# Per-channel constants issued from ScalarE's DMA queue instead of SyncE's in the opening of a one-layer hybrid trunk

## The chip, the cores and the metric

The kernel runs on one core of a Trainium2 chip. A core has five engines that run side by side: TensorE (matrix products, PE in the profile, with its weight loads listed as PEld), VectorE (DVE), ScalarE (ACT), GpSimd (POOL) and SyncE (SP). Each engine takes its own instructions in order. Data moves between the DRAM and the on-chip memory by DMAs. SP, ACT and POOL can issue a DMA; the issue occupies the issuing engine's queue (SPq, ACTq, POOLq in the profile) for a moment, and the data arrives, or "lands", later.

The metric is the device time of one execution in microseconds (us), the median of several runs.

## The reference, cut to what matters

One layer of a streaming-encoder trunk, on a sequence of 512 tokens with 1024 channels, in 32-bit floats. The part in which the change lies is the very beginning: the input's normalisation and the first columns of the input projection, which feed the first branch gate.

```
h     = rms_norm(x, norm_mix)                       # 512 x 1024
proj  = h @ w_in                                    # to 8192 columns
u_pool, u_lru, q, k, v, g_logits = split(proj)
gates = sigmoid(g_logits + b_gate)                  # three gates of 1024 channels
y_pool, y_lru, y_sb = pooling, recurrence, attention mixers
merged = sum over the three branches of gate * (y @ w_branch)
x = x + merged @ w_out
x = x + (silu(h2 @ w_gate) * (h2 @ w_up)) @ w_down  # h2 = rms_norm(x, norm_ffn)
```

`rms_norm` divides each token by its root mean square and multiplies each channel by its entry in `norm_mix`.

## The kernel before, in words

Channels lie on the 128 partitions and tokens along the free dimension. The input comes transposed, `xt`, as eight tiles of 128 channels by 512 tokens, called here xt0 to xt7. Nearly every product is made from three: an operand is split into a rounded part ("hi") and its remainder ("lo"), and hi x hi, hi x lo and lo x hi are summed, so a splitting pair of instructions on ACT (hi) and DVE (lo) stands before every weight tile and every activation tile that TensorE reads.

All the small per-channel vectors (norm weights, gate biases, convolution weights, the constants of the recurrence and so on) are packed by the host into one array `vecs`, 128 partitions by 114 numbers. One DMA brings it into the tile `vt`, where every user takes its column with `vcol(name, i)`. The first users are the splitting of the first input tiles (`make_h`, L433 to 439), which scales by a column of `norm_mix`, and `lru_constants` (L539 to 560), a chain of small VectorE instructions with one on GpSimd, whose results are wanted much later.

The opening runs like this. While nothing has landed, TensorE runs nine products on a constant tile (`warm_ps`, L422), whose results nobody reads. SP issues the DMA of `vt` (L447), then per k the tile xt_k (`load_xt`, L431), and the matching piece of weights. The first weight tile `raw0` is loaded in two halves of 256 KB (L450): the half for k = 0 from ACT's queue, the half for k = 1 from SP's. Each half is split by VectorE alone (cast on L451, remainder on L452). `make_h(k)` then makes hi of the scaled input on ACT (L437) and lo on DVE (L438); both read xt_k and `vt`. Later weight tiles of this stage come through `emit_next`, which issues a 512 KB DMA on SP (L117) and splits on ACT (L110) and DVE (L111).

TensorE's first real work is the loop on L701: for each k, twelve products of 128 x 128 by 512 into four accumulators `ps_gate`: four with the hi weights and hi input, four with the lo weights and hi input, four with the hi weights and lo input. For eight k these are 96 products. They need, in this order: hi weights and hi input, lo weights, lo input. After them come the rest of the first gate, the recurrence's columns, the attention, the branch products, the output product and the feed-forward network, all run by TensorE one after another in a fixed order.

The order of the instructions on each engine is laid down when the program is built, by a scheduler that sorts by priorities and its own estimates of when operands come; the hardware then follows this order. A DMA has one of eight completion counters, given out in turn, and the eighth DMA after it waits on its queue until the counter's last DMA has landed.

Of the kernel before, what the change touches and what calls it, by code (L numbers as in the profile page):

```python
# [66 lines left out]
def layer_kernel(ctx: ExitStack, tc: tile.TileContext, x, xt, vecs, w_in, w_qkv7, w_gate7, w_pool, w_rg, w_ig,  # L67
                 w_branch, w_br7, w_out, w_fg, w_fu, w_fd, w_fd7, out):
    nc = tc.nc
# [22 lines left out]
    def cols(ap, k0, nk, c0, nc_):  # L92
        return ap[k0 * P:(k0 + nk) * P, c0:c0 + nc_].rearrange("(k p) c -> p k c", p=P)
# [198 lines left out]
    vt = cst.tile([P, NV], F32, tag="vt", name="vt")  # L292
# [115 lines left out]
    with ExitStack() as first:  # L408
# [21 lines left out]
        def load_xt(k):  # L430
            nc.sync.dma_start(xts[k], xt[k * P:(k + 1) * P, :])  # L431

        def make_h(k):  # L433
            t = t4([2, S], f"hu{k}", F32R)
            hh, hl = t[:, 0, :], t[:, 1, :]
            gcol = vcol("norm_mix", k)
            act(hh, xts[k], AF.Copy, scale=gcol)  # L437
            dve.scalar_tensor_tensor(hl, xts[k], gcol, hh.bitcast(F32), ALU.mult, ALU.subtract)  # L438
            hu.append((hh, hl))
# [4 lines left out]
        raw0 = wp.tile([P, 2, 512], F32, tag="raw", name="raw0")  # L444
        ready["first", 0] = hi0, lo0
        src0 = cols(w_in, 0, 2, 5120, 512)
        nc.sync.dma_start(vt, vecs)  # L447
        for k in range(2):
            load_xt(k)
            (nc.sync if k else nc.scalar).dma_start(raw0[:, k, :], src0[:, k, :])  # L450
            dve.tensor_copy(hi0[:, k, :], raw0[:, k, :])  # L451
            dve.tensor_tensor(lo0[:, k, :], raw0[:, k, :], hi0[:, k, :].bitcast(F32), ALU.subtract)  # L452
            make_h(k)
# [802 lines left out]
    with ExitStack() as ffn:  # L1256
# [18 lines left out]
        for c in range(4):  # L1275
# [10 lines left out]
            for j in range(2):  # L1286
                k = 2 * c + j
# [382 lines left out]
```

## Time and profile before

| what | value |
| --- | --- |
| median of 3 runs | 901.03 us (900.64 to 901.3) |
| the profiled execution's own time | 900.73 us |
| its span in the profile | 899.0 us |
| granted TensorE clock, share of full | 1.0 |
| busy: TensorE products | 893.4 us (99%) |
| busy: VectorE | 732.3 us (81%) |
| busy: ScalarE | 523.2 us (58%) |
| busy: GpSimd | 86.3 us (10%) |

The profile gives for each engine how long it was busy, and for each wait which other engine or DMA ended it. A row of the timeline has a start in us from the beginning of the span, a duration, the engine, the source line, the operation with its output and inputs, and a count when several neighbours were merged. "SPq" and "ACTq" are the queues of SP and ACT, whose rows are the issues of DMAs, not the transfers. "To landing" is the time from the start of an issue to the last arrival. The profiled execution's time is 1.73 us longer than its span and 0.30 us below the median of the runs.

### The profile page before, as it was taken

How to read it: one execution, taken by the hardware profiler on the slowest of the kernel's cores; microseconds unless marked ns; L12 is line 12 of the kernel's file. 1: busy time of each engine (PE TensorE's matmuls, PEld its weight loads, DVE VectorE, ACT ScalarE, POOL GpSimd, SP SyncE). 2: the span in 40 equal slices, each digit the busy share in tenths (PEclk: the TensorE clock that was granted, in tenths of full speed). 3: DMA queues.
4: the chain of work that ended last, by engine and by line, in shares of the span. 5: the costliest groups of instructions: out<-in, count | busy, mean ns of one | idle time of the engine just before them, and what ended most of it. 6: DMA issues, size and time to landing. Idle time of an engine off the chain costs nothing.

```text
span 899.0 us, 14052 instructions
## 1 busy us (share of the span) xinstructions
PE 893.4 (99%) x5491; PEld 794.2 (88%) x5491; DVE 732.3 (81%) x922; ACT 523.2 (58%) x722; POOL 86.3 (10%) x126
## 2 busy tenths in 40 slices
PE   9999999999999999999999999999999999999998
PEld 6888778788899888888888988889999999989998
DVE  7897897988786599967887696699888888799764
ACT  7554989556856556555664544454555555664532
POOL 1110002232332101000001100000000000101200
PEclk9999999999999999999999999999999999999999
DMA  9585347789682785734736865245543333866842
GB/s 337 147 303 156 115 127 215 234 286 242 181 260 71 233 235 190 220 118 141 223 91 152 184 177 170 94 131 152 141 117 95 111 102 125 225 167 122 180 99 94
DMA packets 116579, 151.98 MB, mean 169 GB/s; under 512 B 8096, under 2 KB 90016, under 8 KB 116512
## 3 DMA queue, kind: packets, MB, share of 16 engines
q1 hardware_dynamic: 104416, 107.30, 37.7%
q0 software_dynamic: 11952, 43.52, 20.6%
q8 instruction: 43, 0.70, 0.3%
q10 hardware_dynamic: 144, 0.26, 0.1%
q14 instruction: 24, 0.20, 0.1%
HBM read 130.61 MB, written 18.87 MB: 166 GB/s over the span
## 4 chain that ended last, share of the span: by engine, by line
PE 95%; DVE 2%; ACT 2%; issue 1%; DMA 0%; SPq 0%; DVEq 0%; ACTq 0%
PE ps_y L287 11%; PE ps_x L287 8%; PE ps_q L798 7%; PE ps_dy L287 5%; PE ps_dx L287 4%; PE ps_br L278 3%; PE ps_br L279 3%; PE ps_br L280 3%; PE ps_gate L701 2%; PE ps_bY L1238 2%; PE ps_gy L287 2%; PE ps_gate L280 2%; PE ps_bX L1238 2%; PE ps_gx L287 2%; PE ps_gate L279 2%; PE ps_gate L278 2%
## 5 line engine op out<-in xcount | busy, mean ns | idle before, releaser
L110 ACT ACTIVATE whi<-raw 128x1024 fp32r<-128x1024 f32 x73 | 77.2, 1058 | 85.3 <-PE ps_out L279 17.0
L111 DVE TENSOR_TENSOR wlo<-raw,whi 128x1024 fp32r<-128x1024 f32 x73 | 89.1, 1220 | 32.9 <-ACT whi L110 32.9
L111 DVE TENSOR_TENSOR wlo<-qw,whi 128x1024 fp32r<-128x1024 f32 x48 | 58.6, 1222 | 20.8 <-ACT whi L110 20.5
L110 ACT ACTIVATE whi<-qw 128x1024 fp32r<-128x1024 f32 x48 | 50.8, 1057 | 33.1 <-PE ps_q L798 18.6
L1403 ACT ACTIVATE wh_S<-w_S 128x1024 fp32r<-128x1024 f32 x36 | 38.2, 1064 | 35.5 <-PE ps_y L287 22.4
L1404 DVE TENSOR_TENSOR wl_S<-w_S,wh_S 128x1024 fp32r<-128x1024 f32 x36 | 43.8, 1220 | 6.2 <-ACT wh_S L1403 6.2
L1403 ACT ACTIVATE wh<-w 128x1024 fp32r<-128x1024 f32 x27 | 28.8, 1066 | 30.3 <-issue 11.9
L1494 POOL DMA_DIRECT2D dw<-in_w_down_dram x16 | 13.5, 846 | 325.9 <-DVE wl L1404 248.2
L1404 DVE TENSOR_TENSOR wl<-w,wh 128x1024 fp32r<-128x1024 f32 x27 | 32.9, 1220 | 10.0 <-ACT wh L1403 10.0
L1403 ACT ACTIVATE whdS<-dw 128x1024 fp32r<-128x1024 f32 x16 | 17.0, 1064 | 24.4 <-PE ps_dy L287 13.2
L1404 DVE TENSOR_TENSOR wldS<-dw,whdS 128x1024 fp32r<-128x1024 f32 x16 | 19.6, 1224 | 12.9 <-ACT whdS L1403 12.9
L1054 DVE TENSOR_TENSOR_SCAN E<-K,ahead 128x512 f32<-128x512 f32 (+3 forms) x32 | 25.3, 812 | 4.4 <-ACT K L1050 4.4
L278 PE MATMUL ps_br<-yHH,whi 128*128 128x512 f32 x64 | 25.3, 395 | 0.0
L278 PE MATMUL ps_lru<-HH,whi 128*128 128x512 f32 x64 | 25.2, 394 | 0.0
L278 PE MATMUL ps_br<-yph,whi 128*128 128x512 f32 x64 | 25.2, 394 | 0.0
L278 PE MATMUL ps_pool<-HH,whi 128*128 128x512 f32 x64 | 25.2, 393 | 0.0
L279 PE MATMUL ps_br<-ypl,whi 128*128 128x512 f32 x64 | 25.0, 391 | 0.0
L280 PE MATMUL ps_gate<-HH,wlo 128*128 128x512 f32 x64 | 25.0, 391 | 0.0
L278 PE MATMUL ps_gate<-HH,whi 128*128 128x512 f32 x64 | 25.0, 391 | 0.0
L280 PE MATMUL ps_br<-yph,wlo 128*128 128x512 f32 x64 | 25.0, 391 | 0.0
L279 PE MATMUL ps_br<-yHL,whi 128*128 128x512 f32 x64 | 25.0, 390 | 0.0
L279 PE MATMUL ps_pool<-HL,whi 128*128 128x512 f32 x64 | 25.0, 390 | 0.0
(717 smaller groups left out, 3426.3 us busy)
## 6 DMA issues: line engine op xcount, KB each, us to landing
raw<-in_w_in_dram SPq DMA_DIRECT2D x31, 512.0 KB, 5.2
qw<-in_w_qkv_dram SPq DMA_DIRECT2D x24, 512.0 KB, 6.8
w<-in_w_ffn_gate_dram SPq DMA_DIRECT2D x36, 256.0 KB, 4.1
w<-in_w_ffn_up_dram SPq DMA_DIRECT2D x36, 256.0 KB, 4.6
raw<-in_w_branch_dram SPq DMA_DIRECT2D x16, 512.0 KB, 4.4
dw<-in_w_down_dram POOLq DMA_DIRECT2D x16, 512.0 KB, 6.3
qw<-in_w_qkv_dram POOLq DMA_DIRECT2D x12, 512.0 KB, 7.6
qd<-r POOLq DMA_DIRECT2D x12, 512.0 KB, 7.2
```

The source lines that it names most:

```text
L110: act(hi, raw, AF.Copy)
L111: dve.tensor_tensor(lo, raw, hi.bitcast(F32), ALU.subtract)
L278: nc.tensor.matmul(ps, lh, rh, start=start, stop=False, skip_group_check=skip)
L279: nc.tensor.matmul(ps, lh, rl, start=False, stop=False, skip_group_check=skip)
L280: nc.tensor.matmul(ps, ll, rh, start=False, stop=stop, skip_group_check=skip)
L287: nc.tensor.matmul(o, a_[a][:, w, k, :], b_[b][:, k, :], start=first and n == k == 0, stop=last and n == 2 and k == 3, skip_group_check=True)
L701: nc.tensor.matmul(pss[n // 2][n % 2], w[:, k % 2, n * P:(n + 1) * P], hu[k][x_], start=k == 0 and w is wh and x_ == 0, stop=k == KT - 1 a ...
L798: nc.tensor.matmul(ps[:, a, :], b_[:, k, ts_], a_[:, kk, :], start=first and n == k == 0, stop=n == 2 and k == 3, skip_group_check=True)
L1054: dve.tensor_tensor_scan(E[:, c0:c0 + n][:, ::-1], K[:, c0 + 1:c0 + n + 1][:, ::-1], ahead[:, S - n:][:, ::-1], 0.0, ALU.mult, ALU.add)
L1238: nc.tensor.matmul(o, ah[x_][:, w, k, :], b[k][y_], start=first_ and n == k == 0, stop=n == 2 and k == 3, skip_group_check=True)
L1403: act(h, src, AF.Copy)
L1404: dve.tensor_tensor(l, src, h.bitcast(F32), ALU.subtract)
```

## The change

The DMA that loads `vt` is taken from the head of SP's queue and placed on ACT's queue, behind the DMA of the first half of `raw0`. SP's queue then begins with xt0. No tile, size or computation is changed.

```diff
         src0 = cols(w_in, 0, 2, 5120, 512)
-        nc.sync.dma_start(vt, vecs)
         for k in range(2):
             load_xt(k)
             (nc.sync if k else nc.scalar).dma_start(raw0[:, k, :], src0[:, k, :])
+            if k == 0:
+                nc.scalar.dma_start(vt, vecs)
             dve.tensor_copy(hi0[:, k, :], raw0[:, k, :])
             dve.tensor_tensor(lo0[:, k, :], raw0[:, k, :], hi0[:, k, :].bitcast(F32), ALU.subtract)
             make_h(k)
```

In the built program the order on TensorE and GpSimd is the same as before. On ACT one DMA issue stands between the first DMA and the loading of the activation table. On SP the first DMA is gone. On VectorE the first thirty or so instructions are in another order: before, three small instructions of `lru_constants` (L540, L544, L545) stand ahead of the cast of the first half of `raw0` (L451); after, the cast and the remainder (L451, L452) come first, then two of the small ones, then lo of xt0 (L438), the cast of the second half, lo of xt1, and the remainder of the second half. From the last steps of the `lru_constants` chain on, some forty instructions in, VectorE's order is the same too. A few completion counters change hands: xt5's issue now waits for `vt` to have landed, where the issue of the third weight tile did before.

## The prediction

> **What bounds the kernel now.** I read the page first, for the engines' shares, then TensorE's waits, then its busy time by stretches.
>
> ```profile
> span 899.0 us, 14052 instructions
> PE 893.4 (99%) x5491; PEld 794.2 (88%) x5491; DVE 732.3 (81%) x922; ACT 523.2 (58%) x722; POOL 86.3 (10%) x126
> ```
> ```profile
> PE warm_ps L422 <- DVE warm L301: 1.5, 1, 1.5
> PE ps_gate L701 <- ACT hu L437: 0.5, 1, 0.5
> PE ps_q L798 <- DVE wlo L111: 0.4, 1, 0.4
> ```
> ```profile
> 5.39:27.50 22.11, 22.11 (x97) 18.29 (x98) 17.70 (x48) 15.00 (x28) 1.56 (x2) 1.00 0.90 319
> 27.50:100.00 72.50, 72.50 (x333) 59.12 (x333) 64.67 (x80) 43.94 (x51) 5.00 (x6) 1.00 0.61 194
> 100.00:899.00 799.00, 795.38 (x5055) 715.63 (x5053) 648.00 (x788) 461.92 (x641) 77.08 (x93) 1.00 0.58 162
> ```
>
> TensorE is the bound, and to a rare degree: once the first real product has begun, its only wait that counts is 0.4 us on L798. In the stretches the first two numbers, length and TensorE's busy time, are equal until 100 us. In the last one 3.62 us are missing: that 0.4 us and the end, where TensorE has stopped and the output is stored. The busy 893.4 us contain 3.41 us of dummy products (row below), so the real ones take 893.40 - 3.41 = 889.99. The span is then the time of the first real product, 5.39, plus 889.99, plus 3.62, which gives 899.0. Of these only the 5.39 lies where the change is. So the question is one number: when does the first product on L701 start?
>
> ```profile
> 0.74 0.40 ACTq L450 DMA_DIRECT2D raw<-in_w_in_dram  x1
> 0.74 0.39 SPq L447 DMA_DIRECT2D vt<-in_vecs_dram  x1
> 1.16 1.28 ACT L1268 ACT_TABLE_LOAD   x1 [1.16 <-PEq L1641]
> 1.19 0.90 SPq L431 DMA_DIRECT2D xt<-in_xt_dram  x2
> 1.46 3.41 PE L422 MATMUL warm_ps<-warm 128*128 128x512 bf16 x9 [1.46 <-DVE warm L301]
> 2.12 0.43 SPq L450 DMA_DIRECT2D raw<-in_w_in_dram  x1
> 2.46 0.31 ACT L1268 ACTIVATE onesr<-ones 128x128 fp32r<-128x128 f32 x1
> 3.63 0.15 DVE L540 TENSOR_SCALAR qg<-vt 128x1 f32<-128x1 f32 x1 [2.23 <-DMA vt<-in_vecs_dram]
> 3.98 0.42 DVE L451 CAST whi<-raw 128x512 fp32r<-128x512 f32 x1
> 4.62 1.53 ACT L437 ACTIVATE hu<-xt,vt 128x512 fp32r<-128x512 f32 x2 [1.85 <-DMA xt<-in_xt_dram]
> 5.39 1.21 PE L701 MATMUL ps_gate<-hu,whi 128*128 128x512 f32 x4 [0.53 <-ACT hu L437]
> ```
> ```profile
> 1.19 3.35 DMA xt<-in_xt_dram
> 4.62 0.73 ACT hu L437
> 5.39 22.10 PE ps_gate L701 x96
> ```
>
> The timeline of the opening and the chain that ended last tell the same story. xt0 is issued at 1.19 and lands 3.35 later, at 4.54. ACT makes hi of it (0.73 us) and TensorE starts at 5.39, which is 0.85 after the landing. The other two inputs were earlier: `vt` lets VectorE go at 3.63, and the cast weights end at 3.98 + 0.42 = 4.40. So xt0 is last, `vt` has some 0.9 us to spare, and the change trades one for the other.
>
> **The change part by part.** Prices of the transfers, size and time to landing (medians of issues of the same kind):
>
> ```profile
> xt<-in_xt_dram SPq DMA_DIRECT2D x8, 256.0 KB, 6.1
> raw<-in_w_in_dram ACTq DMA_DIRECT2D x1, 256.0 KB, 3.1
> raw<-in_w_in_dram SPq DMA_DIRECT2D x1, 256.0 KB, 4.5
> vt<-in_vecs_dram SPq DMA_DIRECT2D x1, 57.0 KB, 2.9
> ```
>
> *Removed from SP's queue.* One issue. The next began 1.19 - 0.74 = 0.45 later, so xt0, xt1, the second half of `raw0` and the tiles after them are issued 0.45 us earlier. xt0 becomes a first DMA of 256 KB at 0.74. Its nearest row is `raw0`'s first half, also 256 KB and first on its queue: 3.1, so xt0 lands near 3.84; with its old 3.35 it would be 4.09. If that were all, TensorE would start 0.45 to 0.70 earlier.
>
> *Added to ACT's queue.* One issue after `raw0`'s, at 0.74 + 0.45 = 1.19, the place that xt0 had on SP. ACT's table load and the activation on `ones` move from an end at 2.77 to 3.22; ACT then idled 1.85 us until xt0, so 1.40 of that cover is left and the cost is nothing. Without the cover it would be the 0.45.
>
> *`vt`'s landing, the term that decides.* ACT's first hi needs `vt` too. The trace has no `vt` behind another DMA, so I bound it. Below: its own 2.9, which gives 1.19 + 2.9 = 4.09, as if the 256 KB ahead of it cost nothing. Above: 4.5, the dearest of the rows of the opening's first DMAs, which gives 5.69. Between them I count bytes. When xt0 landed at 4.54, what had been moved ahead of it or with it was `vt`, `raw0`'s half and xt0: 57 + 256 + 256 = 569 KB. In the changed kernel what is ahead of `vt` or with it is `raw0`'s half, xt0 and `vt`: the same 569 KB. So 4.54 again, plus whatever part of xt1, now waiting on SP's queue behind xt0, is served beside `vt`. All of xt1, 262 kB at the 337 GB/s of the first slice of the page, is 0.78 us:
>
> ```profile
> GB/s 337 147 303 156 115 127 215 234 286 242 181 260 71 233 235 190 220 118 141 223 91 152 184 177 170 94 131 152 141 117 95 111 102 125 225 167 122 180 99 94
> ```
>
> I take half of it, 0.39, since neither none nor all has a row: `vt` lands at 4.93, still nearer to the row of xt0 than to either end. With the same 0.85 from landing to product, TensorE starts at 5.78 instead of 5.39: +0.39. The ends give 4.09 + 0.85 = 4.94 (-0.45) and 5.69 + 0.85 = 6.54 (+1.15).
>
> [...]
>
> *VectorE's new order.* The cast and remainder of `raw0`'s first half no longer stand behind the small instructions that wait for `vt`. They were not late (4.40 against 5.39), so this gains nothing. The first small instruction that needs `vt` now stands ahead of lo of xt0, which needs ACT's hi, itself behind `vt`; no new wait. The cast of the second half moves ahead of lo of xt1:
>
> ```profile
> 5.38 1.56 DVE L438 SCALAR_TENSOR_TENSOR hu<-xt,vt,hu 128x512 fp32r<-128x512 f32 x2 [0.25 <-ACT hu L437]
> 6.85 0.42 DVE L451 CAST whi<-raw 128x512 fp32r<-128x512 f32 x1
> 9.02 1.06 ACT L110 ACTIVATE whi<-raw 128x1024 fp32r<-128x1024 f32 x1 [0.78 <-DMA raw<-in_w_in_dram]
> 10.12 1.23 DVE L111 TENSOR_TENSOR wlo<-raw,whi 128x1024 fp32r<-128x1024 f32 x1 [0.56 <-ACT whi L110]
> 11.69 0.87 PEld L701 LDWEIGHTS ps_gate<-hu,wlo 128*128 128x128 f32 x4
> ```
>
> That cast may wait for the half's landing, 2.12 + 4.5 = 6.62 before and about 0.45 sooner after. It ended at 7.27; the twelve products of k = 1 begin 22.1 / 8 = 2.76 after the first, at 8.15, so 0.9 us of cover remains, more if the start slips. Lo of xt1 is wanted last of the three, 8/12 of 2.76 further on. Cost nothing.
>
> *Later tiles.* The tightest supply in the opening is the lo weights for k = 2: ready at 10.12 + 1.23 = 11.35, loaded at 11.69, 0.34 to spare. Their DMA is issued 0.45 earlier and the start is later, so the slack grows. xt5's issue, which now waits for `vt`, was among the three at 5.55 on SP (not quoted), for products near 5.39 + 5 x 2.76 = 19.2; cost nothing.
>
> *Does a later start come through to the end?* The one later wait, on L798, is fed by a chain of ACT and VectorE that hangs on TensorE's own products:
>
> ```profile
> 126.61 0.92 PE lg L626 x6
> 128.25 0.69 ACT li L631
> 166.22 1.13 DVE wlo L111
> 167.39 0.73 PE ps_q L798 x2
> ```
>
> From the products at 126.61 on, ACT and then VectorE run up to the one that TensorE waits for at 167.39. It shifts with TensorE, so it neither absorbs the shift nor adds to it. The whole +0.39 stands: the span goes from 899.0 to 899.4, an execution like the profiled one from 900.73 to 901.1, and, since that lies 0.30 below the median of the runs, a median from 901.03 to **901.4 us**.
>
> **The rivals.**
>
> *The constants are hidden anyway (a gain).* If `vt`, small as it is, slips through at 2.9 from its issue, it lands at 4.09, as xt0 does by 3.84 to 4.09, and TensorE starts at 4.94: 901.03 - 0.45 = 900.6. For it speaks that `vt` landed first of all before; against it that it was then first on its queue, and now 256 KB stand ahead of it. It decides if `vt` lands before 4.54.
>
> *The constants starve behind SP's stream (slower).* SP issues tile after tile without pause. If ACT's queue gets little of the DMA engines beside it, `vt` lands when the stream lets it:
>
> ```profile
> DMA to landing us min/median/max: 3.3/6.1/7.0
> ```
>
> That is the row of the xt tiles; at their worst, 7.0, `vt` would land at 1.19 + 7.0 = 8.19 and TensorE start at 9.04: +3.65, 904.7. It passes 0.2% of the time, 1.8 us, which is about what a measurement of this kernel can tell from no change, once `vt` lands after 4.54 + 1.8 = 6.34. Against it: `raw0`'s half held its own on ACT's queue (3.1) while SP issued four DMAs.
>
> *The dummy products' work is lost (slower).* They warm TensorE:
>
> ```profile
> L422 PE MATMUL warm_ps<-warm x9: 379/634/634, 1.5 to 4.5; 128*128 128x512 bf16 x9
> 2.29 0.15 PEld L422 LDWEIGHTS <-warm 128*128 128x128 bf16 x1 [0.28 <-issue]
> 3.57 0.15 PEld L422 LDWEIGHTS <-warm 128*128 128x128 bf16 x1 [0.28 <-issue]
> ```
>
> Weight loads at 2.29 and 3.57, three products apart, make 0.43 us a product, against 22.10 / 96 = 0.23 on L701. TensorE was idle 0.53 us between the two; now it would be 0.53 + 0.39 = 0.92, and nothing shows that the fast pace survives that. If it fell back for as long as the slow stretch at the start, about 1.46 to 4.0, the 2.54 us would do 5.9 products worth 1.36 at the fast pace: 1.18 lost, 901.4 + 1.2 = 902.6. It decides at an unknown idle time above 0.53.
>
> [...]
>
> **How the numbers follow.** Forecast, `vt` last and TensorE 0 to 1.15 later: 0.66. Constants hidden, a gain of up to 0.45: 0.14. Starved: 0.08. Pace lost: 0.05, half of it past 1.8 us with a late `vt`. What I don't see: 0.07, of which 0.03 faster, 0.025 same and 0.015 slower. No change to within 0.2% is 0.66 + 0.14 + 0.025 + 0.025 = 0.85, slower 0.08 + 0.025 + 0.015 = 0.12, faster 0.03. A gain past 1.8 us has no room in the trace, as the bounds stop at -0.45. The range runs from 901.03 - 0.45 and 0.2 for the spread of the runs, 900.4, to 901.03 + 1.15 and 0.3 toward the lost pace, 902.5. That leaves out the starved case, most of the unseen and a part of the lost pace, under 2 in 10.
>
> **What would show it.** In the changed profile, ACT's first hi (L437) is to be released by `vt`, no longer by xt0, near 4.9 to 5.0; the first product on L701 near 5.8; TensorE's idle time before it near 0.9. xt0 itself is to land near 3.8 to 4.1. From there to 27 us TensorE shows no gap. The prediction is wrong if L437 starts before 4.5 or after 6.4, if the products on L701 run at 0.43, or if a wait of TensorE appears later that isn't there now.

## The result, and the profile after

The changed kernel takes 902.05 us in the median of 19 runs, against 901.03 for the kernel before in 19 runs beside it. The ratio is 1.0016, with a 95% interval from 1.0009 to 1.0023: slower, by an amount just under the 0.2% that the prediction took for the bound of what can be told; the interval reaches a little over it. The times themselves say more than the median:

| 19 runs each | lowest | median | highest | above 902.5 us |
| --- | --- | --- | --- | --- |
| before | 900.48 | 901.03 | 902.26 | 0 |
| after | 901.56 | 902.05 | 904.44 | 7 |

The whole distribution is about 1.0 us higher, and seven executions are another 0.7 to 2.6 us above the median of the other twelve (901.89). The profiled execution is the highest of the 19, 904.44 us, so its profile shows both parts and more than a typical run has.

Page and waits of TensorE in the kernel after:

```profile
span 902.7 us, 14052 instructions
PE 896.4 (99%) x5491; PEld 795.8 (88%) x5491; DVE 732.4 (81%) x922; ACT 523.1 (58%) x722; POOL 86.3 (10%) x126
```
```profile
PE ps_gate L702 <- ACT hu L437: 1.0, 1, 1.0
PE ps_q L799 <- DVE wlo L111: 0.4, 1, 0.4
PE pq L1019 <- DMA at<-qd: 0.2, 1, 0.2
```

TensorE is busy 3.0 us longer with the same 5491 products, and its wait before the first real one has grown from 0.5 to 1.0. (Lines behind the change are numbered one higher than before.) The timeline of the opening:

```profile
0.74 0.39 ACTq L449 DMA_DIRECT2D raw<-in_w_in_dram  x1
0.74 0.89 SPq L431 DMA_DIRECT2D xt<-in_xt_dram  x2
1.16 0.45 ACTq L451 DMA_DIRECT2D vt<-in_vecs_dram  x1
1.46 4.02 PE L422 MATMUL warm_ps<-warm 128*128 128x512 bf16 x9 [1.46 <-DVE warm L301]
4.96 0.43 DVE L452 CAST whi<-raw 128x512 fp32r<-128x512 f32 x1 [3.56 <-DMA raw<-in_w_in_dram]
5.68 1.33 ACT L437 ACTIVATE hu<-xt,vt 128x512 fp32r<-128x512 f32 x2 [2.44 <-DMA vt<-in_vecs_dram]
6.46 2.07 PE L702 MATMUL ps_gate<-hu,whi 128*128 128x512 f32 x4 [0.98 <-ACT hu L437]
8.33 1.91 PE L702 MATMUL ps_gate<-hu,wlo 128*128 128x512 f32 x4
10.04 2.42 PE L702 MATMUL ps_gate<-hu,whi 128*128 128x512 f32 x8
12.29 1.09 PE L702 MATMUL ps_gate<-hu,wlo 128*128 128x512 f32 x4
```

ACT's first hi is now released by `vt`, as forecast, but `vt` lands 4.4 after its issue, at 5.60, and TensorE starts at 6.46, which is 1.07 later. The products that follow are slow: the second group of four begins 1.87 after the first and the third 1.71 after that, 0.43 to 0.47 a product. Before, the same stretch read:

```profile
6.45 1.09 PE L701 MATMUL ps_gate<-hu,wlo 128*128 128x512 f32 x4
7.37 1.99 PE L701 MATMUL ps_gate<-hu,whi 128*128 128x512 f32 x8
9.20 1.07 PE L701 MATMUL ps_gate<-hu,wlo 128*128 128x512 f32 x4
```

The group that began at 9.20 begins at 12.29 now: 3.09 later, of which 1.07 is the start and 2.02 the pace. The span grew by 902.7 - 899.0 = 3.7. Product by product, the distance between the two traces is 3.12 from the thirtieth on, stays there to within 0.05 for three hundred microseconds, and grows by 0.57 around 309 us (in the time of before), where TensorE waits for a tile `at` that comes late (the row `pq` above); there is no such wait in the profile of before.

### The profile page after: what moved, and what is told of

Its sections match the earlier page's. It is cut to its first block, busy times and chain, and to the rows that moved or that the text cites. A ratio compares the mean times of both kernels' runs of the same rounds, so it can differ in the third digit from the quotient of the medians.

```text
span 902.7 us, 14052 instructions
## 1 busy us (share of the span) xinstructions
PE 896.4 (99%) x5491; PEld 795.8 (88%) x5491; DVE 732.4 (81%) x922; ACT 523.1 (58%) x722; POOL 86.3 (10%) x126
## 4 chain that ended last, share of the span: by engine, by line
PE 93%; DVE 2%; ACT 2%; DMA 2%; issue 1%; SPq 0%; ACTq 0%; DVEq 0%
PE ps_y L287 11%; PE ps_x L287 8%; PE ps_q L799 7%; PE ps_dy L287 5%; PE ps_dx L287 4%; PE ps_br L278 3%; PE ps_br L279 3%; PE ps_br L280 3%; PE ps_gate L702 3%; PE ps_bY L1239 2%; PE ps_gy L287 2%; PE ps_gate L280 2%; PE ps_bX L1239 2%; PE ps_gate L278 2%; PE ps_gate L279 2%; PE ps_lru L278 2%
```

## The experiments

Each was timed beside the kernel before on the same chip. In the first four that had 27 runs, median 900.96; in the last four 33 runs, median 901.19. The theory tested had two terms: a late start in every execution, and a lost pace in some.

**The changed kernel again.** No edit beyond the change itself.

> The changed kernel once more, for a second profile and more times. Theory A (two terms: the constants land near 5.6, so the first product starts 1.0 to 1.1 later in every execution; on top of it, in a part of the executions, TensorE stays at 0.43 us a product for some ten products, another 2 us): the first product again between 6.2 and 6.6, the lowest time about 1.0 above the lowest of before, the times spread over 2 us or more. Theory B (the profiled execution was a stray one, and the constants normally land near 4.9): the first product near 5.8 and the lowest time 0.4 above that of before.

Median 901.67 of 11 runs (900.89 to 903.45), ratio 1.0011, interval 1.0003 to 1.002. The chain that ended last:

```profile
1.17 4.50 DMA vt<-in_vecs_dram
5.76 0.73 ACT hu L437
```
```profile
6.53 2.08 PE L702 MATMUL ps_gate<-hu,whi 128*128 128x512 f32 x4 [1.05 <-ACT hu L437]
8.40 1.71 PE L702 MATMUL ps_gate<-hu,wlo 128*128 128x512 f32 x4
9.95 2.00 PE L702 MATMUL ps_gate<-hu,whi 128*128 128x512 f32 x8
```

`vt` lands at 5.67 and the first product starts at 6.53, so the first profile was no stray in its start, and the second theory is out. The products are slow again, for the first seven or eight this time. Three of the 11 runs are above 903.2, the other eight below 902. The lowest time, 900.89, is only 0.4 above that of before (the next is 901.43), less than the 1.0 that the first theory had; the median is 0.7 above. Both profiles of the changed kernel are of executions with the slow products (904.44 and 903.44), so the start of a typical execution was not profiled.

**13 dummy products.**

```diff
-WARM = 9
+WARM = 13
```

> The changed kernel with 13 dummy products instead of 9, which fill TensorE's idle time before the first real product. Theory A (the idle time costs the fast pace in a part of the executions): the spread shrinks to that of before, under 1.5 us, the highest times go, the first real product starts no earlier than in the changed kernel (6.2 to 6.6) but runs at 0.23 us a product within a few products; median 0.3 to 1.0 below that of the changed kernel in the same call. Theory B (the pace does not depend on that gap): median and spread as in the changed kernel, or later by the length of the added products that overrun, up to 0.6.

Median 901.98 (901.30 to 903.74), ratio 1.001, interval 1.0001 to 1.0019. On the times the theory's expectation failed: neither the median nor the spread came down. The trace shows part of what was expected:

```profile
1.46 5.73 PE L422 MATMUL warm_ps<-warm 128*128 128x512 bf16 x13 [1.46 <-DVE warm L301]
6.63 1.67 PE L702 MATMUL ps_gate<-hu,whi 128*128 128x512 f32 x4
8.13 1.09 PE L702 MATMUL ps_gate<-hu,wlo 128*128 128x512 f32 x4
```

The first four products took 1.50, the next ones run at 0.23, so the pace came within the first product or two and not after ten. All 13 dummy products were slow in this execution, and the last of them, begun at 6.56, stands ahead of the first real one; `vt` landed at 5.68, so the start could be no earlier than some 6.53 in any case. Filling the gap shortened the slow stretch in this profile; that it is worth anything in the times was not shown. This execution took 903.01, one of the two highest of 11. By product, 1.23 of its distance from the kernel before is the start and 0.46 the slow products; another 0.67 comes after 820 us and is not explained.

**The constants first on ACT's queue, the weight half second.**

```diff
+        nc.scalar.dma_start(vt, vecs)
         for k in range(2):
             load_xt(k)
             (nc.sync if k else nc.scalar).dma_start(raw0[:, k, :], src0[:, k, :])
-            if k == 0:
-                nc.scalar.dma_start(vt, vecs)
```

> ACT's two DMAs in the other order: the constants first, the first weight half second; SP still begins with xt0. Theory A (the constants were late because 256 KB stood ahead of them on their queue): they land again 2.9 to 3.1 after their issue, near 3.7; the weight half, now second, becomes the last input at 4.9 to 5.3, its cast ends 0.45 later, and the first product starts at 5.4 to 5.8; times within 0.0 to 0.5 above before. Theory B (whatever is issued in the first microsecond lands late when two big transfers start together, since the DMA engines are slow at the very start): the constants land after 4.2 although first, and the first product starts at 6.0 or later.

```profile
3.92 0.72 ACT L437 ACTIVATE hu<-xt,vt 128x512 fp32r<-128x512 f32 x1 [0.66 <-DMA vt<-in_vecs_dram]
```
```profile
5.34 0.43 DVE L451 CAST whi<-raw 128x512 fp32r<-128x512 f32 x1 [0.77 <-DMA raw<-in_w_in_dram]
```
```profile
5.91 1.17 PE L701 MATMUL ps_gate<-hu,whi 128*128 128x512 f32 x4 [0.56 <-ACT hu L437]
```
```profile
vt<-in_vecs_dram ACTq DMA_DIRECT2D x1, 57.0 KB, 3.2
raw<-in_w_in_dram ACTq DMA_DIRECT2D x1, 256.0 KB, 4.1
```

Median 901.34 (900.89 to 902.22), ratio 1.0003, interval 0.9994 to 1.0012: 0.38 above before, and the interval holds 1. First on its queue, `vt` lands 3.2 after its issue, a little over the 2.9 to 3.1 of the first theory, and ACT makes its first hi at 3.92. xt0 has landed by then, 3.0 after its issue by the trace, so here it did come early. Now the weight half is last: its cast ends at 5.77 and TensorE starts at 5.91, a little past the 5.4 to 5.8 expected. (The profile names ACT as releaser, whose second hi happens to end at 5.86; the first had long been done.)

**xt1 held back.** Three DMAs of one number each between xt0 and xt1 on SP's queue, first into a new small tile:

```diff
         for k in range(2):
+            if k == 1:
+                dum = cst.tile([P, 4], F32, tag="dum", name="dum")
+                for i in range(3):
+                    nc.sync.dma_start(dum[0:1, i:i + 1], vecs[0:1, i:i + 1])
             load_xt(k)
```

> The changed kernel with three DMAs of one number each on SP between xt0 and xt1, which hold xt1 and all behind it back by some 1.3 us, so that the constants have no tile of SP's stream beside them. Theory A (xt1 shares the DMA engines with the constants): they land 0.4 to 0.8 earlier than in the changed kernel, at 4.8 to 5.2, and the first product starts at 5.7 to 6.1. Theory B (the 512 KB of the first weight half and xt0 ahead of them set their landing, and a slow start): they land within 0.2 of the changed kernel, near 5.5, and the first product stays at 6.3 to 6.5.

Median 908.55 of 4 runs (908.3 to 908.81), ratio 1.0083, interval 1.0069 to 1.0097. The opening did what the first theory said:

```profile
vt<-in_vecs_dram ACTq DMA_DIRECT2D x1, 57.0 KB, 3.7
```
```profile
5.77 1.19 PE L706 MATMUL ps_gate<-hu,whi 128*128 128x512 f32 x4 [0.78 <-ACT hu L437]
```

`vt` lands 3.7 after its issue instead of 4.4 and 4.5, and TensorE starts 0.69 and 0.76 earlier than in the two profiles of the changed kernel. The median is 7.6 above before. By product, the distance from the kernel before is 0.38 at the start and 1.4 at the fortieth product, after a wait for late lo weights at 13 us; the other 6.4 grow between 50 and 580 us and are none of the opening's.

**The same without moving a tile.** The three numbers go into the padding tile that the kernel has anyway.

```diff
-    cst.tile([P, PAD], F32, tag="pad", name="pad")
+    pad = cst.tile([P, PAD], F32, tag="pad", name="pad")
...
+            if k == 1:
+                for i in range(3):
+                    nc.sync.dma_start(pad[0:1, i:i + 1], vecs[0:1, i:i + 1])
```

> The changed kernel with the three small DMAs between xt0 and xt1 again, but written into a padding tile that nobody reads, so that no tile's place in memory moves. Expected of the opening, by the earlier run: the constants land at 4.8 to 5.1 and the first product starts at 5.7 to 5.9, later tiles hold TensorE up by 0.2 to 0.6. If the seven microseconds that the earlier run lost after the opening came from the moved tiles, they are gone and the median is 0.6 to 1.3 above before; if they came from the late stream, it stays near 908.

```profile
vt<-in_vecs_dram ACTq DMA_DIRECT2D x1, 57.0 KB, 3.6
```
```profile
PE ps_gate L705 <- ACT hu L437: 0.2, 1, 0.2
PE ps_gate L705 <- DVE wlo L111: 0.2, 1, 0.2
```
```profile
1.46 4.02 PE L422 MATMUL warm_ps<-warm 128*128 128x512 bf16 x9 [1.46 <-DVE warm L301]
5.66 1.69 PE L705 MATMUL ps_gate<-hu,whi 128*128 128x512 f32 x4 [0.18 <-ACT hu L437]
```

Median 902.99 (902.09 to 903.91), ratio 1.0017, interval 1.0008 to 1.0026. `vt` lands 3.6 after its issue and the first product starts at 5.66, near the other form's 5.77. Of the 7.6 above before, 5.8 are gone, so they came with the added tile. What remains, 1.8 above before, is more than the 0.6 to 1.3 expected. The profiled execution, 902.14, is one of the lowest of the 11. Its span is 1.4 longer than before's: 0.27 at the start, 0.45 in slow first products (all nine dummies were slow too), 0.45 at the late weight tile of the second row, and 0.3 after the last product. What the higher executions add isn't settled.

**The constants second on SP's queue.**

```diff
             if k == 0:
-                nc.scalar.dma_start(vt, vecs)
+                nc.sync.dma_start(vt, vecs)
```

> The constants on SP, but second, behind xt0 and ahead of xt1; ACT issues only the first weight half. What stands ahead of them is the same 512 KB as in the changed kernel; what differs is that xt1 now comes behind them on their own queue and not beside them. Theory A (xt1's packets beside them made them late on ACT's queue): they land at 4.6 to 5.1 and the first product starts at 5.5 to 5.9, median 0.2 to 0.6 above before. Theory B (ACT's queue has no part in it, second place as such costs it): they land near 5.6 as in the changed kernel, the first product starts near 6.5, median about 1 above before.

```profile
1.19 3.75 DMA vt<-in_vecs_dram
5.03 0.73 ACT hu L437
5.80 6.39 PE ps_gate L702 x27
```

Median 901.33 (901.0 to 903.54), ratio 1.0003, interval 0.9994 to 1.0012: 0.14 above before, under the 0.2 to 0.6 expected, and the interval holds 1. The same 512 KB go ahead of `vt`, from the same two issues, but xt1 stands behind it on its own queue and not beside it on another. It lands at 4.94 instead of 5.60 and 5.67, and TensorE starts at 5.80. In the two runs in which xt1 was held back `vt` landed at 4.91 and 4.80, on ACT's queue; in the run with 13 dummies, whose DMAs are those of the changed kernel, at 5.68. Three landings stand against three, and this shows the cause of the late constants: SP's stream behind xt0, xt1 first, costs them 0.66 to 0.87 when it runs beside them. The runs hold back xt1 and all that follows it, so they don't part the two. For scale, `vt` landed at 3.61 and 3.98 in two profiles with the same DMAs (before, and six dummies below).

**Six dummy products in the kernel before.** No DMA is touched.

```diff
-WARM = 9
+WARM = 6
```

> The kernel before with 6 dummy products instead of 9; no DMA is touched, only TensorE's idle time before the first real product grows, from 0.5 to about 1.4 us. Theory A (an idle time of 1 us and more in the opening keeps TensorE at 0.43 us a product for longer): the first product starts at 5.4 as before, but the products run slowly until 8 to 11.4 us in most or all executions; median 1.2 to 2.5 above before. Theory B (the pace does not depend on that idle time; the changed kernel's slow products have another cause): times as before, within 0.3.

```profile
5.59 2.08 PE L701 MATMUL ps_gate<-hu,whi 128*128 128x512 f32 x4 [1.39 <-ACT hu L437]
7.46 1.77 PE L701 MATMUL ps_gate<-hu,wlo 128*128 128x512 f32 x4
9.06 1.98 PE L701 MATMUL ps_gate<-hu,whi 128*128 128x512 f32 x8
```

Median 902.92 (901.28 to 903.38), ratio 1.0017, interval 1.0008 to 1.0026. With the constants where they were, three dummies fewer and an idle time of 1.39 ahead of the first product are enough for the slow groups (1.87 and 1.60 for four products), and for 1.7 us in the median. So the slow pace of the changed kernel needs no change of the DMAs. The run takes away three products as well as making the idle time longer, and doesn't part the two. In this run's profile xt0 landed at 4.73 and TensorE would have waited there with any number of dummies.

**The columns of the norm first.** The kernel before, with the constants split in two.

```diff
-        nc.sync.dma_start(vt, vecs)
+        nc.sync.dma_start(vt[:, 0:8], vecs[:, 0:8])
...
             make_h(k)
+        nc.scalar.dma_start(vt[:, 8:], vecs[:, 8:])
         load_xt(2)
```

> The kernel before, with the constants split: the eight columns that the first splitting needs (4 KB) stay first on SP's queue, the other 106 columns go to ACT's queue behind the first weight half. Theory A (TensorE's start hangs on the last of xt0, the first weight half and the columns of the norm, and what is ahead of xt0 delays it by its bytes): xt0 lands 0.0 to 0.3 earlier than 4.54, the start moves to 5.1 to 5.4, median 0.0 to 0.3 below before. If 4 KB first on the queue delay xt0 as much as 57 KB, or the rest beside xt0 takes back the gain, the median is within 0.2 of before.

```profile
PE warm_ps L422 <- DVE warm L301: 1.5, 1, 1.5
PE ps_q L799 <- DVE wlo L111: 0.4, 1, 0.4
```
```profile
1.46 4.02 PE L422 MATMUL warm_ps<-warm 128*128 128x512 bf16 x9 [1.46 <-DVE warm L301]
5.44 1.70 PE L702 MATMUL ps_gate<-hu,whi 128*128 128x512 f32 x4
```

Median 900.73 (900.40 to 901.63), ratio 0.9996, interval 0.9988 to 1.0005. This points the right way, 0.46 below before in the median, but the interval holds 1, so a gain isn't shown. In its profile TensorE has no wait ahead of the first product: the dummies were slow throughout and ended as the first product could start. ACT's first hi began at 4.67, against 4.62 before, so xt0 landed no earlier without the 53 KB ahead of it, and the start, 5.44, is no earlier than 5.39. The expected 0.0 to 0.3 at xt0 and the start of 5.1 to 5.4 didn't come, so this profile gives no reason for the lower median.

## Why the prediction was right or wrong

Right: the change makes the kernel slower, by less than 0.2%; 902.05 lies within 900.4 to 902.5 and 0.65 above the 901.4 forecast. That is +1.02 where +0.37 was forecast, so the direction and the path are right and the size is not. ACT's first hi waits for `vt` and no longer for xt0. The start comes through to the end: in the second profile the distance between the traces is 1.14 at the first product and 2.6 after the slow ones, and is still 2.7 at the end. The table load, VectorE's new order and the later tiles cost nothing: no wait of TensorE between its first product and 27 us. The idle time near 0.9 came out as 0.98 and 1.05 by luck: the start was 0.7 later than the forecast 5.78, and slow dummies ended 0.6 later. Two of the prediction's own signs of being wrong came true: the first real products ran at 0.43, and the first profile has a later wait that wasn't there before (the row `pq`).

Wrong, in three places.

*The landing of `vt`: both terms of its sum were too small.* The first term is the 4.54, the landing of xt0 before, which I took over because I counted the same 569 KB in both kernels. With xt1 held back or behind them on their own queue, the constants landed at 4.80, 4.91 and 4.94, so this term was short by 0.26 to 0.40. The count was wrong, too: the trace of the kernel before has 0.85 MB begun by 4.54, which is about xt1's size more. The second term is the 0.39 for the part of xt1 served beside the constants, half of 0.78, for want of a row. Measured, SP's stream beside them costs 0.66 to 0.87. By their landing 1.17, 1.22 and 1.19 MB had begun to move in the three profiles with xt1 beside them, and 0.95, 0.80 and 0.77 in the three without: the difference, 0.2 to 0.45, is about one to nearly two tiles of 0.26 MB. With the constants second on SP the landing was 4.94 and the start 5.80, the forecast's 4.93 and 5.78; that is luck, as the forecast reached them by a base too early and a share of xt1, which here stands behind the constants. The start of the changed kernel lies at the upper end of my 0 to 1.15, which came from the dearest row, 4.5.

All of xt1 beside the constants, the 0.78, would have been nearer than my half of it: the start moved by 1.07 and 1.14. How transfers that run beside each other share the DMA engines, no run here shows.

*The landing of xt0 and of the weight half.* I priced xt0, once first on its queue, at 3.1 to 3.35, and so near 3.84 to 4.09. In the changed kernel the tiles' shortest time to landing, which is that of xt0, was 4.4, and in its second profile 3.8:

```profile
DMA to landing us min/median/max: 4.4/6.2/6.9
```
```profile
DMA to landing us min/median/max: 3.8/5.7/6.4
```

`raw0`'s half rose too, from 3.1 to 4.2 and 4.0. So taking an issue of 0.45 off the head of the queue gave xt0 nothing: it landed at 5.12 and 4.56, against 4.54 before. The price that I took, 3.1, was that of 256 KB beside `vt`'s 57 KB. With `vt` first on the other queue xt0 did land 3.0 after its issue; beside `raw0`'s 256 KB it took 4.4 and 3.8. I had asked what stood ahead of each transfer and not what would stand beside it. This did not set the start: in the second profile xt0 landed 0.56 and the weight half 0.18 earlier than in the first, and `vt` 0.07 later.

*The lost pace.* I gave it 0.05 as one case by my own estimate, which rests on no row, and described it as a fast pace that falls back. It is neither rare nor that. In the changed kernel 7 of 19 runs are above 902.5 and in the second set 3 of 11, against 0 of 19 and 1 of 27 before. The price in the first profile was 2.0, where I had 1.2. And all nine dummy products of that execution were slow: they end at 5.48 after 4.02 us, where before they took 3.41. TensorE had not yet reached its fast pace when the dummies ran out, and after the idle 0.98 it did not reach it before 10.88.

The ten traces show when the fast pace came, execution by execution. Each records the stretch at the full granted clock (the views print 1.00 for the time before it as well), and this stretch begins where the products change from 0.43 us each to 0.22 or 0.23: at 4.12 in the kernel before, among the dummies, and at 10.88 in the changed kernel, among the real products. The table sets beside it when the dummies ended (their start, 1.46, and their time), how long TensorE was then idle, and what the slow real products cost against the kernel before, all in us:

| run | full clock from | dummies end | idle before the first real product | cost |
| --- | --- | --- | --- | --- |
| before | 4.12 | 4.87 | 0.53 | none |
| xt1 held back | 4.37 | 5.00 | 0.78 | none |
| second on SP | 4.88 | 5.25 | 0.55 | none |
| first on ACT | 5.09 | 5.35 | 0.56 | none |
| norm columns first | 6.55 | 5.48 | 0 | 0.46 |
| xt1 held back, padding tile | 6.77 | 5.48 | 0.18 | 0.45 |
| 13 dummies | 7.45 | 7.19 | 0 | 0.46 |
| six dummies | 8.94 | 4.20 | 1.39 | 1.49 |
| changed, again | 9.76 | 5.48 | 1.05 | 1.45 |
| changed | 10.88 | 5.48 | 0.98 | 2.06 |

In the first four the pace was there before the dummies ended, and 0.5 to 0.8 of idle time did no harm. In the other six every dummy was slow, and so were the real products until the full clock came: at 6.55 to 7.45 where TensorE was idle for 0 to 0.18, for a cost of 0.45 or 0.46, and at 8.94 to 10.88 where it was idle for 0.98 to 1.39, for 1.45 to 2.06. Nine slow dummies end at 5.48, which is past the start of the kernel before at 5.39, so there slow dummies bring no idle time, as with the norm columns first. What sets the moment in an execution was not shown: it lies anywhere from 4.12 to 5.09 in four profiles of nine dummies and past their end in four others. That the long idle time itself puts it off is my reading of these ten executions; the run with six dummies changed the idle time and the number of dummies together.

The rival by which the constants slip through unhindered is out: they never landed before 4.8 behind another transfer. Starvation is out too: landings at 5.60 to 5.68 are short of the 6.34 from which it would tell.

The remaining 0.57 of the first profile, at 309 us, was not in the second; what made that tile late was not tried.

## What to carry to other kernels

When a transfer is moved to another queue, count what will be in flight beside it at its new place (0.66 to 0.87 us here), and not only what stands ahead of it: `vt` had 256 KB beside it at the head of a queue, and now had 256 KB ahead and SP's stream of 256 KB tiles on the queue next to it. A small transfer that much work waits for was better first than second here (first on ACT's queue, TensorE started at 5.91; second, at 6.46 and 6.53), even though that held a large one back by an issue slot of 0.45 us. Where dummy products are to bring TensorE to its full pace (six of them instead of nine cost 1.7 us in the median here), a gap behind them was harmless once the full pace had come (up to 0.8 us here), and where it had not, the executions with gaps of 1.0 to 1.4 us lost 1.5 to 2 us to slow products, so the dummies should last until it has come or until the first real product. More dummies alone didn't make the changed kernel measurably faster. A median hides such a loss in a part of the executions, so look at all the times.

## What the runs showed that I had not expected

With a tile of 16 bytes per partition added among the first tiles, and three small DMAs into it, the kernel was 7.6 us slower (908.55 against 900.96), while the same three DMAs into a tile that was already there left it 1.8 slower. The busy time by stretches shows one of the stretches in which it was lost, the form with the added tile first and then the other:

```profile
100.00:300.00 200.00, 200.00 (x1031) 168.28 (x1030) 159.82 (x162) 144.97 (x186) 47.05 (x50) 1.00 0.63 190
```
```profile
100.00:300.00 200.00, 199.63 (x1052) 169.93 (x1051) 161.34 (x164) 145.95 (x187) 46.81 (x50) 1.00 0.65 192
```

TensorE is busy nearly all the time in both, at the full granted clock, but gets 1031 products done instead of 1052, 2% fewer. From 580 us on no more is lost. The added tile moves the places of later tiles, and that is the likely cause, but no run moved places alone, and the mechanism was not tried. Whoever adds a small tile for an experiment should write into one that exists.
